# A hybrid decoder layer on one core: the third head pair's queries moved ahead of a group of seven products, and a longer wait before attention scores

## The chip, the cores and the metric

The kernel runs on one core of a Trainium2 chip. The metric is the device time of one execution in microseconds (us); less is better. The five engines that appear below are TensorE (PE: matmuls and transposes; PEld: its weight loads), VectorE (DVE), ScalarE (ACT), GpSimd (POOL) and SyncE (SP, here only an issuer of DMAs).

## The reference, cut to what matters

One layer for 256 tokens and a model width of 2048, all in float32. Two token mixers read the same normed input, and their outputs are merged by gates. The edit touches branch B (attention) and the products of the merge gates, and leaves every product as it is.

```python
h = rms_norm(x, pre_norm_w)
proj = h @ w_in                      # one projection, split into the parts below
# A: gated DeltaNet, 8 heads of 128, chunks of 64: conv, silu, l2 norm, delta rule
oa = gated_delta_rule(qa, ka, va, beta, g)
oa = rms(oa) * gdn_norm_w * silu(za);          u_a = oa @ w_branch_a
# B: causal attention, 8 heads of 128 (256 tokens are one block)
ob = moba_attention(qb, kb, vb) * silu(moba_z); u_b = ob @ w_branch_b
merged = sigmoid(gate_a) * u_a + sigmoid(gate_b) * u_b
out = x + rms_norm(merged @ w_out, post_norm_w)
```

## The kernel before, in words

**Products in parts.** A float32 operand is split into a high part (rounded on ScalarE, `hi_`, line 222) and a rest (VectorE, `lo_`, line 223), and three products of parts make one product. Weights come in tiles of 512 KB (`raw_`, four buffers) by DMAs that SP issues. The normed, transposed input lies in `hT` for the whole kernel.

**Projections of a head pair.** `proj_t` (line 339) projects two heads at a time, in four tiles of weights, and stops halfway once, so that a half can be placed by itself: two tiles, 32 matmuls. `attention(p)` (line 1157) returns four such pieces for pair p: `queries_half`, `queries_end`, `keys_half`, `keys_end`. The ends copy and add the two halves of each PSUM bank (line 461 on ScalarE, 462 on VectorE), giving `y_mq` and `y_mk`; the keys are also scaled by a row (line 1177). Then `keys_end` queues `attend` for both heads.

**Groups of seven.** The gate product `ga` (1024 of 2048 columns at a time) and the later products are done by a scheme of Strassen's kind. `seven` (line 811) makes seven products p1 to p7 of single quarters, on weights X and Y that GpSimd fetches (1 MB each) and on sums of them (`onto`, VectorE, line 830; `add`, accumulating DMAs, line 826), into four PSUM banks "11", "12", "21", "22". A product of the seven is 24 matmuls and has two splits for them, where a piece of a projection has two splits for 32 matmuls. The rest of the same two column blocks is done plainly by `plains` (line 928), as four fills of 48 matmuls each, one group later.

**`unit`** (line 919) lays out a group of seven with its fills between the products: `p1, a, p5, b, p3, p6, p2, c, p7, (fetch of the next X), d, p4, (fetch of the next Y)`, where a to d are the fills cut into four nearly equal parts by rounding. Before the change the first group has four fills, the pieces of `attention(2)`, so one each; the second has eight, four of `plains` and the four pieces of `attention(3)`, so two each; the third has four of `plains`.

**Queues of small work.** The smaller stages are generators in queues (`gq` for the delta rule, `vq`, `mq`, `aq` with one for each head of a pair, `bq`, `dq`). After every eight matmuls of a projection, or six of a product, `tick` (line 124) goes through the queues, and each generator whose wait has run out puts its next step into the program. A tick takes half a unit off a wait. TensorE's instructions stay in exactly this order (`pin`); those of the other engines are put in order by the framework's planner.

**`attend`** (line 1107), for one head: wait of `A_WAIT1`; scores into a PSUM tile `ms`, scale and mask, row maximum, exponential; wait of `A_WAIT2`; transposes into `pp`, copy to `pT`; wait of `A_WAIT3`; product with the values into `po`, weighting into `zm` (line 1137). `turned_attention` follows after `A_WAIT4` (transposes into `pt`). For heads 4 to 7 it also waits until all eight heads are through.

**The delta rule at that time.** The triangular inverse (line 623) is the last stage before the first group. It fetches the first X and Y (line 673) and reads its own result back through DRAM (`inv`, line 678). While the first group runs, `completed` (`it`, `iw`, `ir`) and `solve` (`sv`, `so`, then the square roots of line 1033, the normalisation of line 1038 and the transposes `ot`) go through `gq`. All PSUM tiles, of whatever stage, come from one pool of eight banks (line 114).

Of the kernel before, what the change touches and what calls it, by code (L numbers as in the profile page):

```python
# [31 lines left out]
SV_WAIT = 1  # L32
OS_WAIT = 2
IN_WAIT = 2
A_WAIT1 = 1
A_WAIT2 = 3
A_WAIT3 = 2
A_WAIT4 = 4
# [32 lines left out]
def hybrid_layer(  # L71
# [44 lines left out]
    def bank(name):  # L116
        return psum.tile([P, 512], F32, tag="bank", name=name)
# [221 lines left out]
    def proj_t(col, name):  # L339

        pts = [bank(f"a_{name}_{m}") for m in range(2)]
        for kb in range(4):
            raw = wraw.tile([P, 4, 256], F32, tag="raw", name=f"raw_{name}_{kb}")
            nc.sync.dma_start(
                raw, w_in[kb * 512 : (kb + 1) * 512, col : col + 256].rearrange("(k p) c -> p k c", p=P)
            )
            hi, lo = split(raw, [P, 4, 256], f"{name}_{kb}")
            for kk in range(4):
                k = kb * 4 + kk
                for m in range(2):  # L350
                    ms = slice(m * P, (m + 1) * P)
                    mm(pts[m], hi[:, kk, ms], hT[:, k, :], start=(k == 0), stop=False)
                    mm(pts[m][:, :S], lo[:, kk, ms], hT[:, k, :S], start=False, stop=(k == KT - 1))
                if kk % 2 == 1:
                    tick()
            if kb % 2:
                yield pts
# [101 lines left out]
    def halves(pt, name):  # L459
        y = wk.tile([P, S], F32, tag="f256", bufs=8, name=f"y_{name}")  # L460
        nc.scalar.copy(y, pt[:, S:])
        nc.vector.tensor_tensor(y, pt[:, :S], y, op=ALU.add)
        return y
# [284 lines left out]
    def product(a, raws, banks, first, name, neg=False, also=None):  # L748

        for u in range(2):  # L750
            raw = raws[u]()
            hi, lo = split(raw, [P, 2, 512], f"{name}_{u}", neg)
            if also:
                also(u, raw)
            for kk in range(2):
                k = 2 * u + kk
                for st, pt, new in zip(a, banks, first):
                    ah, al = st[k]
                    mm(pt, ah, hi[:, kk, :], start=(new and k == 0), stop=False, skip_group_check=True)
                    mm(pt, ah, lo[:, kk, :], start=False, stop=False, skip_group_check=True)  # L760
                    mm(pt, al, hi[:, kk, :], start=False, stop=(k == 3), skip_group_check=True)
                if len(a) > 1 or kk:
                    tick()
# [4 lines left out]
    def quarters(x):  # L768


        def quarter(t, h):
            ks = slice(4 * h, 4 * h + 4)
            return stationary(x[:, ks, t * P : (t + 1) * P], x[:, ks, S + t * P : S + (t + 1) * P])

        return quarter
# [13 lines left out]
    def load(w, h, c, name):  # L789
        def half(u):  # L790
            def f():
                raw = wraw.tile([P, 2, 512], F32, tag="raw", name=f"raw_{name}{c}_{h}_{u}")
                nc.sync.dma_start(raw, piece(w, h, c)[:, 2 * u : 2 * u + 2])
                return raw

            return f

        return half(0), half(1)
# [120 lines left out]
    def unit(sv, fills, following, cuts=None):  # L919

        p1, p5, p3, p6, p2, p7, p4 = sv["p"]
        n = len(fills)
        cuts = cuts or [round(n * i / 4) for i in range(5)]
        a, b_, c_, d = (fills[cuts[i] : cuts[i + 1]] for i in range(4))
        for f in (p1, *a, p5, *b_, p3, p6, p2, *c_, p7, following["x"], *d, p4, following["y"]):
            f()

    def plains(sv, w, c, quarter, name, end):


        def fill(i, h):
            def f():
                pts = sv["banks"][f"1{i + 1}"], sv["banks"][f"2{i + 1}"]
                cc = c + i
                product(
                    [quarter(0, h), quarter(1, h)],
                    load(w, h, cc, name),
                    pts,
                    [False, False],
                    f"{name}{cc}_{h}",  # L940
                    neg=i == 1,
                )
                if h == 3:
                    dq.add(end(cc, pts, i == 1))

            return f

        return [fill(i, h) for i in range(2) for h in (2, 3)]
# [158 lines left out]
    def attend(h, qT, kT):  # L1107
        yield A_WAIT1
        ps = bank(f"ms_{h}")
# [47 lines left out]
    def attention(p):  # L1157
        h = 2 * p
        mqp = proj_t(CMQ + h * P, f"mq{h}")
        mkp = proj_t(CMK + h * P, f"mk{h}")  # L1160
        qTs = []

        def queries_half():
            next(mqp)

        def queries_end():
            pq = next(mqp)
            qTs.extend(halves(pq[m], f"mq{h + m}") for m in range(2))

        def keys_half():  # L1170
            next(mkp)

        def keys_end():
            pk = next(mkp)
            kTs = [halves(pk[m], f"mk{h + m}") for m in range(2)]
            for m in range(2):
                nc.vector.tensor_tensor(kTs[m], kTs[m], rrow, op=ALU.mult)
            for m in range(2):
                aq[m].add(attend(h + m, qTs[m], kTs[m]))

        return queries_half, queries_end, keys_half, keys_end
# [25 lines left out]
    w_ga, w_gb = w_in[:, CGA : CGA + D], w_in[:, CGB : CGB + D]  # L1207
    quarter = quarters(hT)
# [11 lines left out]

    sv1 = seven(w_ga, 0, quarter, hsum, "ga0", None)
    sv2 = seven(w_ga, 2, quarter, hsum, "ga2", None)
    unit(sv1, attention(2), sv2)

    def first_branch(c):
        def times(cc, t, neg):
            def f(pt):
                if neg:
                    nc.vector.scalar_tensor_tensor(ga(cc, t), pt, -1.0, ga(cc, t), op0=ALU.mult, op1=ALU.mult)
                else:  # L1230
                    nc.vector.tensor_tensor(ga(cc, t), ga(cc, t), pt, op=ALU.mult)

            return f

        return {"11": times(c, 0, False), "12": times(c + 1, 0, True), "21": times(c, 1, False), "22": times(c + 1, 1, True)}
# [2 lines left out]
        return quarters(homes["oa"])(t, h)  # L1238

    sv3 = seven(wa, 0, quarter_oa, osum, "ua0", first_branch(0))  # L1240
    unit(sv2, plains(sv1, w_ga, 0, quarter, "ga", sigmoid_gate) + list(attention(3)), sv3)
    while len(osum) < 4:
        gq.tick()
    gq.drain()
# [275 lines left out]
```

## Time and profile before

| | |
|---|---|
| median of 3 runs | 776.99 us (776.87 to 779.88) |
| profiled execution | 774.79 us, its span 773.1 us |
| granted TensorE clock | 0.998 |
| DMA traffic | 152.96 MB, mean 198 GB/s |
| first group of seven, with fills | about 343 to 408 us |
| second group | about 409 to 480 us |
| third group | about 481 to 527 us |

The profile is of one execution, and its span goes from the first to the last instruction; times of instructions are counted from the start of the span. In rows of the order of time stand the start in us, the duration in us, the engine and the line, the operation, the tile written and the tiles read, and the shape; a bracket gives the idle time of the engine ahead of it and what ended that. In the code nearly all matmuls go through the helper of line 132, so the tiles tell them apart, not the lines. Buffer numbers are left out of the names.

### The profile page before, as it was taken

Reading aid. Unit: us, or ns where it says so; the run is one execution under the profiler, and the core shown is the slowest. Engines: PE = TensorE matmul, PEld = TensorE weight load, DVE = VectorE, ACT = ScalarE, POOL = GpSimd, SP = SyncE. Lnnn points to the kernel's source line nnn. Section 1 sums busy time; section 2 is a strip of 40 time slices with the busy share of each in tenths; the row PEclk is TensorE's granted clock in tenths of the full one; section 3 lists DMA queues with packets and bytes.
Section 4 is the critical chain, followed back from the end, with each engine's and each line's share of the span. In section 5 each row is a group of like instructions: output and inputs, shape, how many; then the busy total and the mean of one; then the engine's idle time right before and its main releaser. Section 6 shows DMA issues by size and latency. Waiting matters only on the chain.

```text
span 773.1 us, 10874 instructions
## 1 busy us (share of the span) xinstructions
PE 753.8 (98%) x3920; PEld 640.4 (83%) x3920; DVE 624.0 (81%) x981; ACT 474.2 (61%) x708; POOL 56.0 (7%) x83
## 2 busy tenths in 40 slices
PE   8999999999999999999999999999999999999995
PEld 7897998899888888887897788787888888777885
DVE  5998669896978788968669877888887777999965
ACT  5776666567655555545568765666656545776651
POOL 3000001112000000031000100100101000010100
PEclk9999999999999999999999999999999999999999
DMA  8586576557666666587545576747787776588843
GB/s 302 157 235 219 169 225 171 148 152 223 207 182 189 187 193 188 164 257 187 129 156 172 142 226 208 184 152 259 193 292 196 231 227 216 178 236 300 216 139 109
DMA packets 95132, 152.96 MB, mean 198 GB/s; under 512 B 5221, under 2 KB 49382, under 8 KB 94566
## 3 DMA queue, kind: packets, MB, share of 16 engines
q1 hardware_dynamic: 84598, 122.09, 51.9%
q0 software_dynamic: 9296, 28.32, 13.7%
q10 hardware_dynamic: 1184, 1.84, 0.6%
q8 instruction: 31, 0.51, 0.3%
q14 instruction: 23, 0.19, 0.1%
HBM read 149.09 MB, written 3.15 MB: 197 GB/s over the span
## 4 chain that ended last, share of the span: by engine, by line
PE 81%; DVE 9%; DMA 4%; ACT 3%; issue 3%; POOL 0%; DVEq 0%; ACTq 0%; POOLq 0%
PE a_gb L132 9%; PE a_y L132 8%; PE a_ga L132 6%; PE a_zg L132 6%; PE a_v L132 6%; PE a_zm L132 6%; PE a_ub L132 6%; PE a_k L132 6%; PE a_mq L132 6%; PE a_mv L132 5%; PE a_q L132 5%; PE a_mk L132 5%; PE a_ua L132 4%; DMA two<-in_w_out_dram 2%; PE s L132 1%
## 5 line engine op out<-in xcount | busy, mean ns | idle before, releaser
L132 PE MATMUL a_gb<-hi_gb,hT 128*128 128x512 f32 x192 | 61.1, 392 | 0.0
L132 PE MATMUL a_zg<-hi_zg,hT 128*128 128x348 f32 (+1 forms) x192 | 47.0, 322 | 0.0
L132 PE MATMUL a_mq<-hT,hi_mq 128*128 128x512 f32 x128 | 46.2, 403 | 0.0
L132 PE MATMUL a_mk<-hT,hi_mk 128*128 128x512 f32 x128 | 46.2, 402 | 0.0
L132 PE MATMUL a_q<-hT,hi_q 128*128 128x512 f32 x128 | 45.8, 398 | 0.0
L132 PE MATMUL a_v<-hT,hi_v 128*128 128x512 f32 x128 | 45.6, 400 | 0.0
L132 PE MATMUL a_ga<-hi_ga,hT 128*128 128x512 f32 x128 | 42.7, 397 | 0.0
L132 PEld LDWEIGHTS a_gb<-hi_gb,hT 128*128 128x128 f32 x192 | 36.1, 188 | 7.4
L132 PE MATMUL a_k<-hT,hi_k 128*128 128x512 f32 x128 | 40.5, 399 | 0.9 <-ACT hi_k L275 0.9
L132 PE MATMUL a_zm<-hi_zm,hT 128*128 128x512 f32 x128 | 40.8, 393 | 0.0
L132 PE MATMUL a_ub<-hi_ub,obT 128*128 128x512 f32 x128 | 40.4, 389 | 0.0
L132 PE MATMUL a_mv<-hi_mv,hT 128*128 128x512 f32 x128 | 40.2, 391 | 0.0
L132 PE MATMUL a_gb<-lo_gb,hT 128*128 128x512 f32 x96 | 37.4, 389 | 0.0
L132 PE MATMUL a_mq<-hT,lo_mq 128*128 128x256 f32 x128 | 35.9, 281 | 0.7 <-DVE lo_mq L223 0.7
L132 PE MATMUL a_v<-hT,lo_v 128*128 128x256 f32 x128 | 36.0, 281 | 0.0
L132 PE MATMUL a_q<-hT,lo_q 128*128 128x256 f32 x128 | 35.9, 280 | 0.0
L132 PE MATMUL a_mk<-hT,lo_mk 128*128 128x256 f32 x128 | 35.9, 280 | 0.0
L132 PEld LDWEIGHTS a_zg<-hi_zg,hT 128*128 128x128 f32 x192 | 33.5, 188 | 0.1
L132 PE MATMUL a_zg<-lo_zg,hT 128*128 128x348 f32 (+1 forms) x96 | 30.9, 321 | 0.0
L132 PE MATMUL a_y<-hi_y,mT 128*128 128x512 f32 x96 | 30.8, 393 | 0.0
L132 PEld LDWEIGHTS a_v<-hT,hi_v 128*128 128x128 f32 x128 | 24.1, 188 | 5.8
L132 PEld LDWEIGHTS a_mq<-hT,hi_mq 128*128 128x128 f32 x128 | 24.0, 188 | 5.6
(435 smaller groups left out, 2240.0 us busy)
## 6 DMA issues: line engine op xcount, KB each, us to landing
raw_gb<-in_w_in_dram SPq DMA_DIRECT2D x24, 512.0 KB, 4.6
raw_q<-in_w_in_dram SPq DMA_DIRECT2D x16, 512.0 KB, 4.4
raw_mv<-in_w_in_dram SPq DMA_DIRECT2D x16, 512.0 KB, 3.7
raw_v<-in_w_in_dram SPq DMA_DIRECT2D x16, 512.0 KB, 4.0
raw_zm<-in_w_in_dram SPq DMA_DIRECT2D x16, 512.0 KB, 3.6
raw_mq<-in_w_in_dram SPq DMA_DIRECT2D x16, 512.0 KB, 3.9
raw_mk<-in_w_in_dram SPq DMA_DIRECT2D x16, 512.0 KB, 3.9
raw_ga<-in_w_in_dram SPq DMA_DIRECT2D x16, 512.0 KB, 4.1
```

Of the source, the lines that this page charges most:

```text
L132: return pin(nc.tensor.matmul(*args, **kwargs))
```

## The change

The queries of the third head pair (`attention(2)`, its first two pieces) are put ahead of the first group. That group's four fills are then the keys of the third pair and the queries of the fourth. The second group keeps four plain fills and has two more, the keys of the fourth pair; its six fills are cut into parts of 2, 1, 1 and 2. `A_WAIT1` goes from 1 to 2, for all four pairs.

```diff
-A_WAIT1 = 1
+A_WAIT1 = 2
...
     sv1 = seven(w_ga, 0, quarter, hsum, "ga0", None)
     sv2 = seven(w_ga, 2, quarter, hsum, "ga2", None)
-    unit(sv1, attention(2), sv2)
+    m2, m3 = attention(2), attention(3)
+    for f in m2[:2]:
+        f()
+    unit(sv1, m2[2:] + m3[:2], sv2)
...
     sv3 = seven(wa, 0, quarter_oa, osum, "ua0", first_branch(0))
-    unit(sv2, plains(sv1, w_ga, 0, quarter, "ga", sigmoid_gate) + list(attention(3)), sv3)
+    unit(sv2, plains(sv1, w_ga, 0, quarter, "ga", sigmoid_gate) + list(m3[2:]), sv3)
```

Counted from the end of the second pair's keys to the end of the second group, the program has the same pieces before and after in another order, 76 ticks in both.

## The prediction

> **What bounds the kernel now.** I read the page first (busy times, then the chain that ended last), then the waits of TensorE, and then the order of time on TensorE, VectorE and ScalarE between 340 and 530 us, where the edited groups of seven run.
>
> ```profile
> span 773.1 us, 10874 instructions
> PE 753.8 (98%) x3920; PEld 640.4 (83%) x3920; DVE 624.0 (81%) x981; ACT 474.2 (61%) x708; POOL 56.0 (7%) x83
> PE 81%; DVE 9%; DMA 4%; ACT 3%; issue 3%; POOL 0%; DVEq 0%; ACTq 0%; POOLq 0%
> ```
>
> The reader is to see a kernel that waits for TensorE: 98% of the span busy, 81% of the last chain. The change takes no matmul away and adds none. So it can only win or lose in the gaps between TensorE's instructions, and these are short:
>
> ```profile
> PE ms L132 <- DVE y_mk L1177: 1.5, 2, 1.2
> ```
>
> This is the longest of TensorE's waits (total us, times, longest): `ms`, the attention scores, waits twice for keys (`y_mk`), for pair 1 and pair 3 (a pair is two heads). In order of time on TensorE, the idle in brackets, with the shorter ones of the same stretch, where query projections (`a_mq`) and gate products (`a_ga`) wait for a split:
>
> ```profile
> 343.15 0.40 PE L132 MATMUL a_ga<-hi_ga0p,hT 128*128 128x512 f32 x1
> 343.38 0.40 PE L132 MATMUL a_ga<-lo_ga0p,hT 128*128 128x512 f32 x1
> ...
> 347.24 1.55 PE L132 MATMUL ms<-y_mk,y_mq 128*128 128x128 f32 x8 [1.18 <-DVE y_mk L1177]
> ...
> 352.48 0.39 PE L132 MATMUL a_mq<-hT,lo_mq 128*128 128x256 f32 x1 [0.69 <-DVE lo_mq L223]
> ...
> 413.02 0.50 PE L132 MATMUL a_ga<-lo_ga,hT 128*128 128x512 f32 x1 [0.37 <-DVE lo_ga L223]
> 431.55 0.50 PE L132 MATMUL a_ga<-lo_ga,hT 128*128 128x512 f32 x1 [0.28 <-DVE lo_ga L220]
> 480.13 1.55 PE L132 MATMUL ms<-y_mk,y_mq 128*128 128x128 f32 x8 [0.32 <-DVE y_mk L1177]
> ```
>
> A matmul lasts 0.40 us but the next starts 0.23 us behind it (343.15 to 343.38), so a pause costs its idle plus 0.16: scores 1.34 and 0.48, `lo_mq` 0.85, `lo_ga` 0.53 and 0.44. That is 3.64 us, all that the edit can reach here. What VectorE did before the first two:
>
> ```profile
> 343.75 1.22 DVE L223 TENSOR_TENSOR lo_mq<-raw_mq,hi_mq 128x1024 fp32r<-128x1024 f32 x1
> 344.88 1.22 DVE L830 TENSOR_TENSOR two<-two,raw_ga0t 128x1024 f32<-128x1024 f32 x1
> 346.02 0.75 DVE L462 TENSOR_TENSOR y_mk<-a_mk,y_mk 128x256 f32<-128x256 f32 x2
> 346.68 0.75 DVE L1177 TENSOR_TENSOR y_mk<-y_mk,rrow 128x256 f32<-128x256 f32 x2
> 347.35 1.22 DVE L830 TENSOR_TENSOR two<-two,raw_ga0t 128x1024 f32<-128x1024 f32 x1
> 348.48 0.34 DVE L1115 SCALAR_TENSOR_TENSOR s<-ms,qscale,mask_m 128x128 f32<-128x128 f32 x1
> ...
> 350.89 0.41 DVE L1118 TENSOR_REDUCE mx<-s 128x1 f32<-128x256 f32 x1
> ```
>
> The keys that the scores need stood behind a split and a sum (`two`) of the first product of the seven, p1, and behind the scores came another sum and the softmax, 2.7 us (348.48 to 351.21), which pushed back the `lo_mq` that TensorE wanted at 351.6.
>
> **The change, part by part.** The program's order is counted in ticks; one is eight projection matmuls, or six matmuls of a product at 0.23:
>
> ```profile
> 360.22 2.81 PE a_mq L132 x16
> ```
>
> so 1.40 or 1.38 us. A wait of 1 ends at the second tick after it is queued, a wait of 2 at the fourth.
>
> *Pair 2's queries ahead of p1.* Counted from the end of pair 1's keys: before, ticks 1-2 are p1, 3-6 the first half of the queries, 7-8 p5. After, 1-8 are both halves of the queries, 9-10 p1, 11-14 keys, 15-16 p5, 17-20 keys, 21-26 p3, p6, p2, 27-30 pair 3's queries, 31-32 p7, 33-36 queries, 37-38 p4. Pair 1's scores move from tick 2 to tick 4, that is 2 x 1.4 = 2.8 us later, and the sums of p1 move from there to tick 10. The keys' four instructions, 1.5 us by 346.02 and 346.68, have then only `lo_mq` splits beside them in 5.6 us. The 1.34 us goes. The softmax then finds splits made ahead, so I let the 0.85 us go too. What is late next: the inverse's transposes stay at tick 7, now inside the queries, at about 343.15 + 7 x 1.4 + 1.4 (scores) = 354.4 instead of 356.63.
>
> ```profile
> L678 POOL DMA_DIRECT2D inv<-t_d x4: 697/707/726, 342.5 to 344.6; - x4
> ...
> DMA to landing us min/median/max: 3.2/3.3/3.9
> ```
>
> Their loads, issued by 344.6 and landed 3.9 us later at most, are there by 349, so nothing is added. The DMAs on SP that move with the queries are four of 512 KB; they pass two of p1's (`right`), which are read later too, and POOL's fetches of X and Y were issued before either. I cost these moves at nothing, covered by three ticks at least.
>
> *Wait of two units.* All four pairs' scores come two ticks later, and so do their `pp`, `po` and for pairs 2 and 3 the order of what follows. Pair 3's 0.48 us goes (its keys get 5.6 us instead of 2.8). Nothing else queues behind them in that attention queue; the turned outputs end by tick 97 of a third group that ends at 106. A pause of the turned outputs at 497 (its row stands below, under PSUM) moves with them, and I leave it as it is. Sum so far: 1.34 + 0.48 + 0.85 = 2.67 us gained.
>
> *Second group with six fills instead of eight.* One projection half goes between its products where two went. VectorE carries that:
>
> ```profile
> 355.14:384.00 28.86, 28.86 (x213) 24.12 (x212) 20.14 (x23) 16.63 (x23) 2.49 (x2) 1.00 0.59 137
> 384.00:405.20 21.20, 21.20 (x142) 19.29 (x141) 13.60 (x25) 14.16 (x45) 1.58 (x2) 1.00 0.47 146
> 405.20:442.80 37.60, 36.90 (x180) 29.73 (x179) 34.84 (x58) 29.28 (x45) 2.44 (x2) 1.00 0.52 160
> ```
>
> Columns: length, then busy us of PE, PEld, DVE, ACT, POOL. Before 405 VectorE has 16 us to spare, behind it 2.8. Pair 2's key work and softmax (1.5 and 2.7 us) leave the full stretch for the slack one. But they come on top of other things there. Ticks 19 to 28 are the second row, 21.2 us with 13.6 of VectorE; after, 1.3 us of scores join them, and for VectorE the 4.2 us of pair 2, two splits and two sums more (p3, p6 and p2 stand there instead of p7 and a projection half), 4.9 at 1.22. That is 22.7 us of VectorE in 22.5 of TensorE: a full stretch moved forward. The nearest row is the third one, as full for longer, and it cost the 0.97 us of `lo_ga`, because splits run ahead of their use. Bounds: the 0.97 gone, or the same again in the new place. I take the 0.97 as it is, so no difference.
>
> *PSUM.* The pool has eight banks (line 114). Pair 3's queries hold two of them in ticks 27 to 36, where before they were held in ticks 57 to 64. At tick 34: 4 for the seven, 2 for the queries, 1 for `ot` of tick 33, and `po` asks for 2, which makes 9. What a full pool costs, and how long an `ot` bank is kept:
>
> ```profile
> 497.42 0.44 PE L135 MATMUL pt<-ident,zm 128*128 128x128 f32 x2
> 499.07 0.44 PE L135 MATMUL pt<-ident,zm 128*128 128x128 f32 x2 [1.22 <-DVE zm L1137]
> ...
> 414.30 0.60 PE L135 MATMUL ot<-ident,oz 128*128 128x128 f32 x4
> ...
> 418.65 0.58 ACT L1063 COPY oa_f<-ot 128x512 f32<-128x512 f32 x1
> ```
>
> I read the second `pt`'s wait as such a one: by the program's order eight banks were held there and a `po` bank comes free by `zm`. `ot` is released at 419.23, 4.3 us after its end at 414.90; the second `po` comes 2.4 us behind its end (0.4 + 1.4 + 0.65), so it lacks 1.9 at worst, 0 if ScalarE copies at once. Three places can meet this (`pp` at tick 30, `po` at 34, `ot` at 35): 0 to 5.7 us. I take half the one wait of that kind, 0.7.
>
> *ScalarE's tables.* The scores of tick 24 put an exponential between two square roots (ticks 23 and 27) which now follow each other.
>
> ```profile
> 394.53 1.28 ACT L1033 ACT_TABLE_LOAD   x1
> ...
> 409.21 1.28 ACT L1119 ACT_TABLE_LOAD   x1
> 410.50 0.40 ACT L1119 ACTIVATE s<-s,mx 128x128 f32<-128x128 f32 x1
> ```
>
> That is one load more, 1.28 us of ScalarE, beside its 14.16 busy of 21.20; I take 0, and 1.28 as the upper bound. The Trainium skill (ScalarE: Activation LUTs, "What ACT_TABLE_LOAD costs") speaks against this edit: functions should be grouped by set, and a switch is 1283 ns and a drain of 1380, 2.66 us in all. The trace agrees with the 1.28 but not with the drain here: the exponential starts 0.01 us behind the load. By the page's full price on the path the sum would be 777.7 instead of 775.0; the rival with the 1.28 stands below.
>
> **Sum.** -2.67 + 0.7 = -2.0 us. The profiled execution took 774.79 us (span 773.1), so it would take 772.8; the median of the three runs is 776.99, 2.2 above it, and gives **775.0**.
>
> **The rivals.** *All gaps close* (20%): no bank is missed and the thinner stretch frees `lo_ga`: -3.64, 773.4 us. For it: 16 us of free VectorE; against: the full ticks 19 to 28. *The waits only move* (15%): the extra table load delays the normalisation and the splits behind it, 1.28, and `lo_ga` doubles, 0.97: -2.0 + 2.25 = +0.3, 777.2 us; this is also how it looks if the edit does not do what it says. *PSUM runs out* (10%), slower: in ticks 30 to 35 each of the three requests waits 1.9 us, 5.7 - 2.67 = +3.0, 780.0 us. It decides against the change from 2.67 us of such waits on, two places at near the full price. Against it: ScalarE is less loaded there than at 414 to 419.
>
> **How the numbers follow.** The forecast has 55%. 0.5% is 3.9 us, about what a measurement of this kernel can tell from no change. Beyond -3.9 lies a good half of the first rival (0.12), since it needs only 0.3 us more than listed; beyond +3.9 half of the third (0.06), if banks also fail at tick 26. The rest, 0.82, is within. The range goes from 772.2 (first rival and 1.2 for the scatter of medians) to 778.5 (second rival and 1.3); outside are the third rival and a little of the first.
>
> **What would show it.** Right: no wait of `ms` for `y_mk` and none of `a_mq` for `lo_mq` near 350; the `pt` wait still there. Wrong: new waits at `po` or `ot` between 400 and 425 that end by ScalarE's `oa_f` or VectorE's `zm` (PSUM), at `a_ga` or `a_mq` by `lo_` splits (VectorE), or at `it` by the loads of `inv`.

## The result, and the profile after

The changed kernel takes 772.28 us (median of 6 runs, 770.13 to 773.61) against 777.58 us (6 runs, 776.23 to 779.88): a ratio of 0.9925, with a 95% interval of 0.9901 to 0.9949. Measured once more later, beside other kernels, it gave 0.9925 (0.9909 to 0.9941). So it is faster by 5.3 to 6 us where 2.0 was forecast. The page of the changed kernel, the lines that answer to those of before:

```profile
span 771.3 us, 10875 instructions
...
PE 753.4 (98%) x3920; PEld 642.8 (83%) x3920; DVE 625.6 (81%) x981; ACT 475.5 (62%) x709; POOL 55.8 (7%) x83
...
PE 89%; DVE 4%; DMA 3%; ACT 3%; issue 2%; POOL 0%; DVEq 0%; ACTq 0%; POOLq 0%
```

The work is the same, the busy times nearly so, and one instruction came in (a table load on ScalarE). In the last chain VectorE has 4% where it had 9%. TensorE's waits in the changed kernel (total us, times, longest):

```profile
PE a_ga L132 <- DVE lo_ga L223: 1.4, 2, 1.1
PE a_y L132 <- DVE lo_y L223: 1.4, 1, 1.4
...
PE po L132 <- ACT oa_f L1063: 0.8, 1, 0.8
...
PE a_y L132 <- DVE lo_y2p L223: 0.8, 1, 0.8
```

No scores (`ms`) wait, no `lo_mq`, no `pt`. New are a `po` that waits for ScalarE, a longer wait for `lo_ga`, and two waits in the output product (`a_y`), far behind the edit.

The two spans differ by 1.8 us, the medians by 5.3. To see what belongs to the edit, I take the stretch from the first matmul of pair 1's keys to the first of the group behind the last place where the order of instructions differs. TensorE before, then after:

```profile
305.83 0.40 PE L132 MATMUL a_mk<-hT,hi_mk 128*128 128x512 f32 x1
...
569.39 0.39 PE L132 MATMUL a_gb<-hi_gb0p,hT 128*128 128x512 f32 x1
```

```profile
306.51 0.40 PE L132 MATMUL a_mk<-hT,hi_mk 128*128 128x512 f32 x1
...
565.05 0.39 PE L132 MATMUL a_gb<-hi_gb0p,hT 128*128 128x512 f32 x1
```

That is 263.56 us before and 258.54 after: 5.0 us gained in the stretch, near the 5.3 of the medians. Behind it the changed kernel's first profile lost 2.5 us in the output product, by instructions that stand in the same order in both, and 0.7 ahead of it (306.51 against 305.83). The experiments look at the gain first and at these losses last.

### The profile page after: what moved, and what is told of

Same layout as the page of the kernel before. It is cut to its first block, busy times and chain, and to the rows that moved or that the text cites. A ratio compares the mean times of both kernels' runs of the same rounds, so it can differ in the third digit from the quotient of the medians.

```text
span 771.3 us, 10875 instructions
## 1 busy us (share of the span) xinstructions
PE 753.4 (98%) x3920; PEld 642.8 (83%) x3920; DVE 625.6 (81%) x981; ACT 475.5 (62%) x709; POOL 55.8 (7%) x83
## 4 chain that ended last, share of the span: by engine, by line
PE 89%; DVE 4%; DMA 3%; ACT 3%; issue 2%; POOL 0%; DVEq 0%; ACTq 0%; POOLq 0%
PE a_ga L132 9%; PE a_gb L132 9%; PE a_y L132 8%; PE a_zg L132 6%; PE a_mk L132 6%; PE a_v L132 6%; PE a_k L132 6%; PE a_mq L132 6%; PE a_zm L132 6%; PE a_ub L132 6%; PE a_mv L132 5%; PE a_ua L132 5%; PE a_q L132 5%; DMA two<-in_w_out_dram 2%; PE s L132 1%
```

## The experiments

Each kernel was timed against the kernel before in the same session; two single executions of the kernel before are named further down.

| kernel | ratio, 95% interval | pauses of TensorE in its profile between 300 and 535 us (idle) |
|---|---|---|
| changed kernel | 0.9925 (0.9901 to 0.9949) | `lo_ga` 1.4, `po` 0.8 |
| wait alone | 0.9938 (0.9923 to 0.9954) | `lo_ga` 1.4, `lo_ga0p` 0.2 |
| order alone | 0.9987 (0.9975 to 0.9999) | `lo_ga` 2.2, `pt` 1.2, `pp` 1.1, `lo_ua2p` 0.5, `ms` 0.2 |
| fourth pair's queries early, alone | 1.0039 (1.0022 to 1.0056) | `lo_mq` 5.4, `ms` 1.9, `pt` 1.2, `pp` 1.2, `lo_ga` 1.1, and `lo_ua2p` 0.7 behind |
| third pair's queries in front, alone | 1.0005 (0.9993 to 1.0017) | `a_ga` for a sum 2.8, `pt` 1.2, `lo_ua2p` 0.5, `lo_ga` 0.5, `ms` 0.3 |
| wait, last pair alone | 0.9959 (0.9946 to 0.9973) | `ms` 1.3, `lo_mq` 0.6, `lo_ga` 0.7 |
| wait, first three pairs | 0.9973 (0.9961 to 0.9986) | `lo_ga` 1.4, `pt` 1.2, `lo_ua2p` 0.6, `ms` 0.3 |
| wait behind the scores | 0.9981 (0.9966 to 0.9995) | `lo_mq` 1.9, `ms` 1.1, `lo_ga` 0.9 |
| changed, all products with values later | 0.9920 (0.9908 to 0.9932) | `po` 0.8 |
| changed, third pair's later | 0.9934 (0.9915 to 0.9952) | `lo_ga` 2.0 |

**The parts of the change.** The first four take it apart.

```diff
 # wait alone: the kernel before with
-A_WAIT1 = 1
+A_WAIT1 = 2
 # order alone: the changed kernel with
-A_WAIT1 = 2
+A_WAIT1 = 1
 # fourth pair's queries early, alone: the kernel before with
-    unit(sv1, attention(2), sv2)
+    m3 = attention(3)
+    unit(sv1, attention(2) + m3[:2], sv2)
...
-    unit(sv2, plains(sv1, w_ga, 0, quarter, "ga", sigmoid_gate) + list(attention(3)), sv3)
+    unit(sv2, plains(sv1, w_ga, 0, quarter, "ga", sigmoid_gate) + list(m3[2:]), sv3)
 # third pair's queries in front, alone: the kernel before with
-    unit(sv1, attention(2), sv2)
+    m2 = attention(2)
+    for f in m2[:2]:
+        f()
+    unit(sv1, m2[2:], sv2)
```

The wait alone:

> The old order, with the scores' wait alone at 2 units. Theory 1 (the gain is the pauses of scores and of the queries' split, as the prediction summed them): the two pauses of the scores go, 1.34 + 0.48, and the rest stays: -1.8 us against the kernel before. Theory 2 (the later scores also move the third group's pause at the turned outputs, 1.38 us, and the late fetch behind it, 0.80 us): -4.0 us, and both pauses are missing from the trace. Theory 3 (the third group gains by the new order of the projections): -1.8 us, both pauses still there.

The order alone:

> The new order, with the scores' wait at 1 unit as before. Theory 1: the pauses near 345 and 351 go (1.34 + 0.85), pair 3's 0.48 stays, and a PSUM pause near 414 comes (1.0): -1.2 to -2.2 us. Theory 2: the same, and the pauses of the third group (1.38 and 0.80) are still in the trace. Theory 3: these two are gone, -3.5 to -4.4 us.

The fourth pair's queries early, alone:

> The old start of the first group (p1 ahead of the third pair's queries) and a wait of 1, but the fourth pair's queries stand in the first group, which has six fills, as the second has. Theories 1 and 2: the pauses near 345 and 351 and those of the third group stay; between -0.5 and +1.0 us. Theory 3: the third group's pauses go, -2.2 us.

The third pair's queries in front, alone:

> The third pair's queries ahead of the first group alone: that group has two fills (the keys), the second has eight as before, the wait is 1. Theories 1 and 2: the pauses near 345 and 351 go, -2.2 us, against which stands what a first group with two fills fewer loses on VectorE, 0 to 3 us; the third group's pauses stay. Theory 3: those stay too, since the second group is not thinner.

The wait alone gives 0.62%, five sixths of the whole; the order alone 0.13%. That fits theory 2 and no other: with the wait, `pt` and `lo_ua2p` are gone, with the order alone both are there, and theory 3 falls with them. Over the stretch that the edit touches, the one profile of the wait alone has the whole gain. Its TensorE:

```profile
307.50 0.40 PE L132 MATMUL a_mk<-hT,hi_mk 128*128 128x512 f32 x1
...
566.01 0.39 PE L132 MATMUL a_gb<-hi_gb0p,hT 128*128 128x512 f32 x1
```

That is 258.51 us, where the changed kernel has 258.54, and the interval of its ratio holds 0.9925 as well. So it is not shown that the new order adds anything to the wait. The order did take away its two pauses near 345 and 351, 2.2 us, and gave nearly all back: `lo_ga` went from 0.7 to 2.2, and `pp` waited 1.1. Both halves of the reordering are worth nothing or less by themselves. With two fills the first group runs out of cover, and its last product, p4, waits 2.8 us for a sum. With six fills and p1 in front, the queries' split waits long in the one profile that there is; its waits from 344 to 360 us:

```profile
ACT hi_mq L222 <- DMA raw_mq<-in_w_in_dram: 7.2, 1, 7.2
...
PE a_mq L132 <- DVE lo_mq L223: 5.4, 1, 5.4
DVE sm L1121 <- ACT s L1120: 4.9, 1, 4.9
```

ScalarE sits in front of a weight tile that has not landed, and the softmax behind it on the same engine waits with it. This tile took 8.3 us from its issue to its landing, and 4.7 at the same place in the kernel before, so the long wait may be chance and not the six fills. I had expected at most 1.0 us of loss here, and the medians differ by 3.0. The profile is of an execution of 783.11 us where the median is 780.93; what the median pays for is not shown. Beside the late tile the profile has 1.2 at `pp`, ended by `oa_f`.

**Which pair, and which step of it.** The next three ask where the wait earns its 4.8 us.

```diff
 # last pair alone: the kernel before with
-        yield A_WAIT1
+        yield A_WAIT1 + (h >= 6)
 # first three pairs: the kernel before with
-        yield A_WAIT1
+        yield A_WAIT1 + (h < 6)
 # behind the scores: the kernel before with
-A_WAIT2 = 3
+A_WAIT2 = 4
```

The last pair alone:

> The old order; the wait of 2 units for the last head pair alone, 1 for the other three. Theory 2, as it stands after the first four runs (the wait moves the last pair's product with the values and its turned outputs in the third group to a place where VectorE does the two heads' weightings back to back and the next weight fetch starts earlier): -3.0 us of the 4.5 that the wait alone gave, and no pause at the turned outputs near 497 nor at the fourth group's first product near 528. Rival (the gain is from the scores themselves, pair 1 most): -0.5 us.

The first three pairs:

> The complement: 2 units for the first three pairs, 1 for the last. Theory 2: -1.5 us (the pauses near 345 and 351 go or shrink), with the pauses near 497 (1.38) and 528 (0.80) in the trace. Rival: -4 us.

The wait behind the scores:

> The old order; the scores' wait at 1 as before, but the wait behind them, ahead of the transposes, at 4 units instead of 3, so that transposes, product with the values and turned outputs come two ticks later and the scores do not. Theory 2: the third group gains 2.2 to 2.6 us by this alone, the pauses of the scores (1.34, 0.48) stay: -2.5 us. Rival (the scores' place decides): 0 to -0.5 us, with the pauses near 497 and 528 in the trace.

The last pair alone gives 0.41%, 3.2 us; the other three 0.27%, 2.1 us. They add up to the wait's 4.8 within their intervals. The larger part is earned in the third group, where the prediction changed nothing but 0.48 us. VectorE there, in the kernel before, in the changed one, and with the last pair's wait alone:

```profile
496.76 0.61 DVE L1137 SCALAR_TENSOR_TENSOR zm<-po,sm,zm 128x128 f32<-128x128 f32 x2 [0.60 <-PE po L132]
497.28 1.22 DVE L223 TENSOR_TENSOR lo_ua0p<-two,hi_ua0p 128x1024 fp32r<-128x1024 f32 x1
498.41 0.61 DVE L1137 SCALAR_TENSOR_TENSOR zm<-po,sm,zm 128x128 f32<-128x128 f32 x2
```

```profile
496.98 1.22 DVE L830 TENSOR_TENSOR two<-two,raw_ua0p 128x1024 f32<-128x1024 f32 x1
498.13 1.19 DVE L1137 SCALAR_TENSOR_TENSOR zm<-po,sm,zm 128x128 f32<-128x128 f32 x4
```

```profile
499.13 1.22 DVE L830 TENSOR_TENSOR two<-two,raw_ua0p 128x1024 f32<-128x1024 f32 x1
500.27 1.18 DVE L1137 SCALAR_TENSOR_TENSOR zm<-po,sm,zm 128x128 f32<-128x128 f32 x4
```

Before, the planner put a split of 1.22 us between the weightings (`zm`) of the two heads, and the second `pt` waited for the second weighting: 1.22 idle, 1.38 with the lost overlap. These turned outputs are those of heads 4 and 5, which the program holds back until all eight heads are through. They read nothing of the new weightings, so what a weighting can give them is the PSUM bank of its `po`. Two ticks later no split falls between the weightings, but that is not what removes the wait. ScalarE and TensorE at that place in the changed kernel:

```profile
497.00 1.27 ACT L1215 ACTIVATE ga<-a_ga,rstd 128x512 f32<-128x512 f32 x2
498.50 0.72 PE L135 MATMUL pt<-ident,zm 128*128 128x128 f32 x4
```

The turned outputs are through at 499.22, before the last weighting is (498.13 + 1.19 = 499.32), so none of them waits for it any more. It is the same in all seven profiles, of six kernels, in which the last pair's `po` comes later; in the seven in which it does not, the wait is 1.2. By the program's order a plain fill ends just there, and the sigmoid of line 1215 has read its two banks by 498.27; in the kernel before, that sigmoid comes only behind the turned outputs (its table load starts at 499.94). That these are the banks that help is my reading of the program; no view names the bank.

The second effect is on GpSimd, which fetches the next X when VectorE has read the old tile (its last split of it ends at 517.08 before and at 512.26 after; the names in the brackets are of instructions that end nearby). The issue of that fetch, before and after:

```profile
517.65 0.80 POOL L821 DMA_DIRECT2D two<-in_w_branch_a_dram  x1 [19.96 <-ACT hi_ga L219]
```

```profile
512.82 0.80 POOL L821 DMA_DIRECT2D two<-in_w_branch_a_dram  x1 [16.52 <-DVE obT L1150]
```

The group that needs it began at 527.17 before and at 524.14 after. So the fetch starts 9.5 us ahead of its use before and 11.3 after. The fetches of that place took 6.5 to 7.1 us to land before and 5.5 after, and two splits follow, so before it comes too late and after it does not. TensorE's waits between 480 and 535 us in the kernel before; the changed kernel has none there:

```profile
PE pt L135 <- DVE zm L1137: 1.2, 1, 1.2
PE a_ua L132 <- DVE lo_ua2p L223: 0.6, 1, 0.6
PE ms L132 <- DVE y_mk L1177: 0.3, 1, 0.3
```

With 0.16 for each that is 1.38, 0.80 and 0.48, 2.66 us together. The wait behind the scores shows that the place of `po` and not that of the scores is what counts here: `pt` and `lo_ua2p` are gone there too, and `ms` still waits. Its 0.19%, 1.5 us, is less than the 2.5 expected, because in the first group `lo_mq` waits longer (1.9 instead of 0.7).

**PSUM, and a faster version.** The wait of `po` in the changed kernel, on TensorE:

```profile
414.25 0.83 PE L132 MATMUL po<-mv,pT 128*128 128x128 f32 x6
415.92 0.82 PE L132 MATMUL po<-mv,pT 128*128 128x128 f32 x5 [0.84 <-ACT oa_f L1063]
```

The second head's `po` reads `mv` and `pT`, nothing of `oa_f`; what ScalarE's copy of `ot` can have set free is the bank. Two kernels move `po`:

```diff
 # all products with values later: the changed kernel with
-A_WAIT3 = 2
+A_WAIT3 = 3
 # third pair's later: the changed kernel with
-        yield A_WAIT3
+        yield A_WAIT3 + 2 * (h // 2 == 2)
```

All of them later by two ticks:

> The changed kernel with the wait ahead of the product with the values at 3 units instead of 2, so that it comes two ticks later, at tick 36 instead of 34 of the first group, when the turned outputs of the delta rule no longer hold a bank that it lacks. If PSUM is what cost the changed kernel 1.0 us near 415: that pause goes, -1.0 us against the changed kernel, so -6.0 to -6.5 against the kernel before. If the third group's gain hangs on the exact tick: its pause of 1.4 comes back, and the result is near -4.

The third pair's alone, by four ticks, when the fourth pair's queries have given back two banks:

> The changed kernel with the third pair's product with the values alone four ticks later, at tick 38, when the fourth pair's queries have given back their two PSUM banks; the other pairs as in the changed kernel. If a lack of banks cost the 1.0 us: no such pause, and -1.0 us against the changed kernel, -1.5 to -2.0 if the gate splits near 430 gain too. If the pause only moves: no difference.

Two ticks later the pause is still there (0.8, now ended by `zm`), four ticks later it is gone. That fits the banks that the queries hold, as the ledger of the prediction had it. It brings no time that the interval shows: `lo_ga` then waits 2.0 us instead of 1.4. The pause is then at a split of VectorE. The first of the two kernels has the best ratio, 0.9920, but the interval holds the changed kernel's 0.9925, so neither is shown to beat it.

**The same kernels again.** What of the two profiles is the kernel, and what is the execution?

The kernel before, a second and a third profile (one execution each, 775.77 and 778.0 us):

> The kernel before, profiled again. If its first profile was a lucky execution (the last weight fetch of the output product came 2.6 us sooner than in the changed kernel's profile, with the same order of instructions): ScalarE waits 1.5 to 3.5 us for that fetch (0.8 in the first profile), the output product pauses 1 to 2.4 us more, and the span is 775 to 777. If the fetch is late because of the change: 0.8 us again, and a span near 773.

> The kernel before, profiled a third time, as for the first of this call: a wait for the last fetch between 0.2 and 3.5 us if that is chance, and near 0.8 if it belongs to the kernel.

The changed kernel:

> The changed kernel again, beside the next one. 0.9925 of the kernel before, as measured; the PSUM pause of about 1.0 us near 415 and the two pauses at gate splits near 430 are there again, the wait for the last fetch 2.5 to 3.5 us.

ScalarE's wait for the last weight fetch of the output product: kernel before, first profile; changed kernel, first profile; changed kernel, second profile.

```profile
ACT hi_y2p L222 <- DMA two<-in_w_out_dram: 0.8, 1, 0.8
```

```profile
ACT hi_y2p L222 <- DMA two<-in_w_out_dram: 3.4, 1, 3.4
```

```profile
ACT hi_y2p L222 <- DMA two<-in_w_out_dram: 0.5, 1, 0.5
```

The same kernel had 3.4 once and 0.5 the other time, and its span was 771.3 and 768.9 us; the kernel before had 0.8, 0.4 and 1.1. The 1.4 and 0.8 us in the output product come with this fetch, and the second profile has neither. That the edit has no part in them is not shown. Behind the stretch the three profiles of the kernel before take 203.6 to 203.9 us. Eight profiles are of kernels with a longer wait; seven of them take 205.2 to 206.2 us there, and only the changed kernel's second takes 203.6, though the instructions stand in the same order. I had expected the kernel before to show the late fetch too, and it did not. What made its first profile quick lies mostly ahead of the stretch, which starts there at 305.83 us and in the other four profiles of the two kernels at 306.51 to 306.81. In the third profile of the kernel before the first group's X came late. Its waits from 338 to 347 us, and TensorE:

```profile
ACT hi_ga0p L222 <- DMA two<-in_w_in_dram: 10.4, 1, 10.4
```

```profile
344.53 0.50 PE L132 MATMUL a_ga<-hi_ga0p,hT 128*128 128x512 f32 x1 [0.23 <-ACT hi_ga0p L222]
345.79 0.50 PE L132 MATMUL a_ga<-lo_ga0p,hT 128*128 128x512 f32 x1 [0.76 <-DVE lo_ga0p L223]
...
350.28 0.89 PE L132 MATMUL ms<-y_mk,y_mq 128*128 128x128 f32 x4 [1.73 <-DVE y_mk L1177]
```

Here p1 stands right behind the keys, and a fetch that lands late holds up p1, the keys' sums behind it and the scores: 0.23 + 0.76 more, and 1.73 at the scores instead of 1.18. The stretch from the keys to the fifth group was 263.56, 263.90 and 265.57 us in the three profiles of the kernel before, 258.54 and 258.56 in the two of the changed one. With the queries in front, X has 14 us more to land, and neither profile shows a wait for it.

## Why the prediction was wrong, point by point

The side was right and the size was not: -2.0 us forecast, -5.3 measured, with 82% put on less than 0.5%.

**The step that failed** is "I leave it as it is", said of the pause of the turned outputs, together with "3.64 us, all that the edit can reach". The list was made from pauses next to moved instructions. It let the 1.38 us at `pt` move along with `po` and `pt` as large as before, and it left out the 0.80 us at the next weight fetch, which stood in the same view of waits with 0.6. My ground for leaving `pt` was a count of eight banks at the old tick, and I did not count again at the new one. What a full pool costs is the time until the next bank comes free. Before, that was set by the split that the planner had put between two `zm`; two ticks later, `pt` no longer waits for the second `zm` in any profile, and a plain fill has ended there. "The `pt` wait still there", which I named as a sign of being right, is the sign that failed. The two pauses make 2.2 of the missing 3.3 us, and the last pair's wait alone shows them at 3.2 with the scores' 0.48.

Two sizes in the description of the kernel are twice too high: a product of the seven has 12 matmuls (343.15 to 345.67 us for p1 in the kernel before), not 24, and a plain fill 24, not 48. The ticks of the prediction are counted with the right ones.

**The fetch of X at p1** was in the sum at nothing, as one of the moves of DMAs, though p1 went eight ticks back. In the profile at hand there was nothing to gain; in one of three profiles of the kernel before it is worth some 2 us.

**Right, and as sized:** the scores' pauses (1.34 and 0.48) and `lo_mq` (0.85) are gone. The PSUM pause came where it was put, at `po` of tick 34 and ended by `oa_f`: 0.84 + 0.16 = 1.0 us. The 0.7 taken was half of one wait, chosen between 0 and 5.7, so that its size came near is in part luck. The inverse's transposes at tick 7 wait for nothing.

**Mis-sized in the other direction:** the full stretch on VectorE was taken as unchanged at 0.97 us of `lo_ga`, with 0.97 more as the bound. In the changed kernel the two are 1.09 and 0.31 idle, 1.72 with the overlap: 0.75 more. The table load came as counted, and its price of 0 on the path stands as far as any wait shows:

```profile
393.97 1.28 ACT L1033 ACT_TABLE_LOAD   x1
...
396.43 1.28 ACT L1119 ACT_TABLE_LOAD   x1
...
404.04 1.28 ACT L1033 ACT_TABLE_LOAD   x1
```

A square root, an exponential, a square root: three loads where there were two. The Trainium skill (ScalarE: Activation LUTs, "What ACT_TABLE_LOAD costs") would have it cost 2.66 us a switch; ScalarE here pays 1.28, and no wait of TensorE ends by it.

**The transfer from profile to median.** 774.79 - 2.0 = 772.8 against a profiled 772.96 looks like a hit and is luck: the profile of before was quicker than any of the six timed runs it was first set beside (776.23 and up), and the first profile after had the late fetch at its end. Compared over the stretch that the edit touches, the same two profiles give 5.0 us where the spans give 1.8: of the difference 2.5 lie behind the stretch and 0.7 ahead of it.

**What stays open:** the named pauses account for 4.85 us gone (1.34, 0.48, 0.85, 1.38, 0.80) and 1.75 come, 3.1 of the 5.0. The rest is in no idle time that the view of waits lists. Over the stretch, before and after (columns as in the prediction):

```profile
305.83:569.39 263.56, 258.68 (x1389) 216.55 (x1388) 214.90 (x316) 165.77 (x256) 23.02 (x26) 1.00 0.65 192
```

```profile
306.51:565.05 258.54, 256.30 (x1388) 217.34 (x1387) 216.38 (x316) 167.14 (x257) 22.93 (x26) 1.00 0.68 195
```

TensorE is busy for 2.4 us less with the same products, of which the overlap lost at four pauses (0.16 each) explains 0.6: the matmuls follow one another a little closer, and why I have not traced. Why the kernel before runs at a median 2.8 us above its first profile is only partly explained, by the late X and by the 0.7 us ahead of the stretch. Whether the late fetch of the output product belongs to the longer wait is open too.

## What to carry to other kernels

When a wait in a hand-made order is changed, follow every step that hangs on it to its end, and price each pause that one of them touches, however far behind the edit; the largest gain here was 150 us behind the first. Where a step asks for a bank of a full pool, count the pool again at the place to which the step moves: a pause does not move along as it is. Time the parts of a change alone; here one number gave five sixths of the gain, and the reordering is not shown to add to it. Compare two profiles over the stretch that the edit can touch, not by their spans alone, and profile the same kernel more than once before a microsecond is put down to a change or to chance.

## What the runs showed that I had not expected

One weight fetch of 1 MB made ScalarE wait 0.5 us in one execution of a kernel and 3.4 in the next, and the span followed by 2.4 us; six other profiles of kernels with a longer wait have the time lost there too. Several kernels that differ by one wait moved pauses of 1 to 2 us from one place to another with nearly no change in time: with VectorE 81% busy over the span, the gain of a removed pause was several times taken by the next one.
